# Probabilities times values: one full-array matmul per head pair in place of two column-tiled ones

## The chip, the core and the metric

The kernel runs on one core of a Trainium2 chip. Its engines are TensorE (PE; its weight loads are listed apart as PEld), VectorE (DVE), ScalarE (ACT), GpSimd (POOL) and SyncE (SP), which run side by side and wait for each other on semaphores. The metric is the device time of one execution in microseconds, less is better; the profile's own clock runs from the first instruction to the last and is called the span.

## What is computed

Two transformer blocks over 512 tokens of width 1024, batch 1, in float32. Two of their parts matter here.

The first block holds a sparse attention with 8 heads of width 64. An indexer chooses 128 keys for each query; the softmax runs over those alone. In the kernel the choice is a bias row (0 or a huge number), so that the products are dense:

```python
logits = jnp.einsum('bqhd,bqkhd->bqhk', qb, kg).astype(jnp.float32) * att_scale
p = jax.nn.softmax(logits, axis=-1).astype(v.dtype)
return jnp.einsum('bqhk,bqkhd->bqhd', p, vg)
```

The second block holds an attention with 8 query heads in 2 groups of 4, each group with one key and one value head of width 64. Its output is a gated sum of three branches: over compressed blocks (32 of them, the last one empty), over selected blocks and over a window. With 512 tokens the last two are plain causal attention with their own keys and values. Beside it stands a gated linear attention (GLA); both go through one output projection (`w_out_2`).

## The kernel before

**Precision.** The large projections (lines 298 to 300, in `mm3`) split both operands into a high and a low part in the type float32r and multiply three times. The attentions' score products of the second block use float32r too; the first block's score products, both blocks' products of probabilities and values, and the retention use plain float32. In the trace each plain float32 matmul is two records, a float32r matmul or a transpose is one.

**An attention** is built by `attend` (line 422): for a tile `t` of 128 queries and each of 4 head pairs `j` it returns three stages. `qk` makes the scores of both heads (line 842 in the first block, 1231 in the second) into PSUM tiles `ps_at` (2 buffers), then takes the row minimum on DVE (439), the exponential on ACT (442) and scales on DVE (449). `tp` transposes the probabilities on PE (419) into `ps_tr` (2 buffers) and copies them on ACT (457) to `pt`. `out` (line 463) multiplies: for each block `cc` of 128 keys and each head `a` of the pair, 64 columns of values are the weights and the 128 transposed probabilities stream past them. Head 0 of the pair uses columns 0 to 63 of PE's array and head 1 columns 64 to 127: two column tiles, listed as `128*64`. Matmuls that use the whole array are listed as `128*128`, those with 64 rows of the array, as line 842's, as `64*128`.

The result of a query tile, `pv()[feature, pair, q]` for all four pairs, fills one PSUM bank (`ps_pv`, one buffer). In the first block, `dsa` (833) copies it to `qaT` in one instruction on ACT (848). In the second, `nsa` (1219) collects three branches in it, the compressed one (`compressed`, line 1283: four matmuls for each query tile with block-diagonal weights `vblk`) and two calls of `attend`, and `split` (360, 361) then writes its high part on ACT and its low part on DVE over the queries, `qS`.

**The order.** `pipeline` (469) runs the stages of the items so that each item's `qk` comes two steps before its `out`. These steps are one task, and `tick` interleaves tasks with the projections: `dsa` runs beside the retention and its projections, `nsa` beside the GLA and its projections. The engines' instruction order is then made by the framework's scheduler from a timeline that it simulates; only in a stretch around lines 666 to 671 is PE's order as written. Each engine runs its list in order.

Of the kernel before, what the change touches and what calls it, by code (L numbers as in the profile page):

```python
# [14 lines left out]
P = 128  # L15
S = 512
# [9 lines left out]
# columns of the packed per-feature vectors  # L26
# [9 lines left out]
# columns of the packed shape-only constants  # L36
# [63 lines left out]
def _layout(inp):  # L100
# [58 lines left out]
    o["wo2"] = tiles(a["w_out_2"][0], KD)  # L159
# [5 lines left out]
class Builder:  # L165
    def __init__(self, nc, tc, ins, out, cdec, dbg=None):
# [5 lines left out]
        self.deep = (4, 3)   # buffers of the attentions' probabilities, and of their transposes  # L172

    # ---------------------------------------------------------------- small helpers
# [32 lines left out]
    def drain(self, t):  # L207
        """the rest of a task"""
# [5 lines left out]
    def tick(self):  # L214
        """emits a share of the work that goes on beside the projections"""
# [31 lines left out]
    def plan(self):  # L247
        """the pieces of the weights in the order of their use"""
# [23 lines left out]
    def ahead(self, n):  # L272
        """starts the next pieces of weights, so that n are ready or on their way"""
# [4 lines left out]
    def load(self, src, pool=None, eng=None):  # L278
        """a piece [128, a, b] of a weight -> its high and low part"""
# [25 lines left out]
    def projA(self, keys, act, ts=slice(0, S)):  # L305
        """out[f, tok] for 128 features, from one or several pieces of k tiles"""
# [19 lines left out]
    def projM(self, keys, act):  # L326
        """projA of three pieces of 8 k tiles, the first half of the tokens before the second"""
# [12 lines left out]
    def projB(self, name, ch, act, evac):  # L340
        """out[tok, n] for a chunk of columns; evac(tok, psum)"""
# [21 lines left out]
    def rsq(self, out, src, scale):  # L363
        """out = (src * scale + eps) ** -0.5 for a few columns"""
# [6 lines left out]
    def tok_sum(self, acc, name):  # L371
        """sums over the features of acc[f, tok] -> [128 tok, 4]"""
# [9 lines left out]
    def bcast(self, col, out):  # L382
        """[128 tok, 4] -> [128, 512], the same in every partition"""
# [20 lines left out]
    def rope(self, x, cos, sin, half, tmp, eng):  # L404
        """rotates x[p, h, 2 * half] in place; sin carries the sign of the first half"""
# [15 lines left out]
    # ---------------------------------------------------------------- attention  # L421
    def attend(self, t, pv, score, vtok, bias, first, rowscale=None):
        """softmax(q k) v of the 8 heads for the queries of tile t, added to pv()[feature, pair, q], as a list of
        stages per head pair. score(psum, h, n) puts out the negated, scaled products with the first n keys"""
# [3 lines left out]
        for j in range(4):  # L428
            Pm, PT, box = [], [], []

            def qk(j=j, Pm=Pm, box=box):
                sm = self.small.tile([P, 2], F32, name="sm", tag="sm", bufs=3)
                for a in range(2):
                    h = 2 * j + a
                    sc = self.ps("at")
                    score(sc, h, n)
# [9 lines left out]
                if rowscale is not None:  # L446
                    nc.vector.tensor_tensor(rs, rs, rowscale(2 * j), op=ALU.mult)
# [3 lines left out]
            def tp(Pm=Pm, PT=PT):  # L451
                for a in range(2):
# [16 lines left out]
    def pipeline(self, items):  # L469
        """the stages of the items, each one item behind the one before"""  # L470
# [16 lines left out]
    # ---------------------------------------------------------------- the whole  # L487
# [67 lines left out]
    def mod_rest(self, lo, hi):  # L555
        """the feature tiles lo .. hi of the modulation"""
# [29 lines left out]
    def norm2(self, acc, ts):  # L586
        """rms(x) * w * (1 + scale) + shift of the tokens ts, split"""
# [20 lines left out]
    # ---------------------------------------------------------------- first block: mixer  # L608
# [109 lines left out]
    def index_proj(self, qi, s0, mods):  # L718
        """the index queries, key and weights; all tiles of tokens grow together, as the feature tiles of h come in"""
# [31 lines left out]
    def index_scores(self, qi, scs):  # L751
# [4 lines left out]
        for t in range(NT):  # L756
# [5 lines left out]
            # the key: high part twice, low part twice; the queries: high and low part of each head  # L762
# [33 lines left out]
    def topk(self, scs):  # L796
        """the 128 largest of each row -> 0, the others -> BIG"""
# [35 lines left out]
    def dsa(self, qaT, kaT, va, scs, tiles):  # L833
        nc = self.nc
        items = []
        for t in tiles:
            bias = self.c("bigmask", 384, 512) if t == 0 else scs[t]
            pv = self.bank()
# [657 lines left out]
```

## Time and profile before

| | |
|---|---|
| median of 3 runs | 1640.35 us (1640.23 to 1642.13) |
| span of the profiled execution | 1638.9 us |
| PE busy | 1600.4 us, 98% of the span |
| PEld, DVE, ACT, POOL busy | 82%, 60%, 43%, 10% |
| granted TensorE clock, mean | 0.996 |
| first attention's line 463 | from 177.8 to 332.2 us |
| second attention's line 463 | from 1054.0 to 1217.2 us |

The profiled execution is one execution; the page gives its span and no time beside it, and the span is 1.45 us under the median of the runs. Matmuls are pipelined, so a record of a matmul is longer than the time that it takes from the next one: what a stretch of matmuls costs is read from where it starts and where the next one starts.

### The profile page before, as it was taken

The page shows a single profiled execution, that of the slowest core. Times are in us where ns is not written, and L with a number is a line of the kernel's source. Part 1 is how long each engine was busy: PE and PEld are TensorE (multiplying, and loading weights), DVE is VectorE, ACT ScalarE, POOL GpSimd, SP SyncE. Part 2 cuts the span into 40 slices and gives each one's busy share as a digit, 9 for nine tenths or more (in the row PEclk, how much of TensorE's full clock was granted, in tenths as well). Part 3 has the DMA queues.
Part 4 walks back from the last instruction along what each step waited for, and adds up shares of the span by engine and source line. Part 5 has one row for each costly group of instructions (what it writes and reads, how often), then busy time and mean ns, then how long its engine had stood idle before and what let it go on. Part 6 is the DMA issues. An engine that isn't in the chain of part 4 may idle for free.

```text
span 1638.9 us, 23692 instructions
## 1 busy us (share of the span) xinstructions
PE 1600.4 (98%) x8941; PEld 1347.3 (82%) x8941; DVE 979.3 (60%) x2233; ACT 696.6 (43%) x1476; POOL 170.1 (10%) x310
## 2 busy tenths in 40 slices
PE   4999999999999999999999999999999999999999
PEld 3899888887888988888888899977778788888887
DVE  7679755557886864443334455675666677777321
ACT  4563656634222642322333334654653444444221
POOL 4431000021110110000000015100110000000000
PEclk9999999999999999999999999999999999999999
DMA  8222221145553633333233353121013222222331
GB/s 320 89 85 90 78 65 40 52 135 180 181 183 118 184 119 123 116 115 104 87 106 108 120 165 98 52 67 50 14 52 103 81 99 90 102 91 87 109 111 53
DMA packets 49297, 173.12 MB, mean 106 GB/s; under 512 B 6032, under 2 KB 6592, under 8 KB 48160
## 3 DMA queue, kind: packets, MB, share of 16 engines
q1 hardware_dynamic: 43232, 152.22, 29.1%
q0 software_dynamic: 5952, 19.40, 3.5%
q8 instruction: 70, 1.15, 0.3%
q14 instruction: 43, 0.35, 0.1%
HBM read 166.88 MB, written 4.19 MB: 104 GB/s over the span
## 4 chain that ended last, share of the span: by engine, by line
PE 96%; DVE 3%; DMA 1%; ACT 0%; issue 0%; POOL 0%; SPq 0%; DVEq 0%; ACTq 0%; POOLq 0%
PE ps_mm L298 27%; PE ps_mm L299 27%; PE ps_mm L300 27%; PE ps_tr L419 4%; PE ps_pv L463 3%; DVE wacc L531 1%; PE ps_at L1231 1%; PE ps_at L842 1%; PE ps_at L1180 1%; PE ps_at L784 1%; PE ps_at L917 0%; PE ps_at L1251 0%; DMA xs<-in_x_dram 0%; PE ps_mm L1413 0%; PE ps_mm L1407 0%
## 5 line engine op out<-in xcount | busy, mean ns | idle before, releaser
L292 ACT CAST wh<-st 128x512 fp32r<-128x512 f32 (+3 forms) x508 | 283.8, 607 | 556.2 <-issue 273.8
L293 DVE TENSOR_TENSOR wl<-st,wh 128x512 fp32r<-128x512 f32 (+3 forms) x502 | 321.3, 670 | 179.5 <-ACT wh L292 178.5
L298 PE MATMUL ps_mm<-hH,wh 128*128 128x512 f32 (+1 forms) x1000 | 393.9, 395 | 4.2 <-DVE us L1458 2.2
L299 PE MATMUL ps_mm<-hL,wh 128*128 128x512 f32 (+1 forms) x1000 | 390.1, 390 | 0.3 <-DVE hL L361 0.3
L300 PE MATMUL ps_mm<-hH,wl 128*128 128x512 f32 (+1 forms) x1000 | 389.0, 389 | 0.0
L298 PEld LDWEIGHTS ps_mm<-hH,wh 128*128 128x128 f32 x1000 | 189.3, 189 | 44.4 <-DVE us L1458 2.4
L300 PEld LDWEIGHTS ps_mm<-hH,wl 128*128 128x128 f32 x1000 | 189.0, 189 | 41.1
L299 PEld LDWEIGHTS ps_mm<-hL,wh 128*128 128x128 f32 x1000 | 189.4, 189 | 38.7 <-DVE hL L361 0.5
L298 PE MATMUL ps_mm<-wh,hH 128*128 128x256 f32 (+2 forms) x672 | 195.9, 294 | 2.5 <-ACT hH L547 2.5
L299 PE MATMUL ps_mm<-wl,hH 128*128 128x256 f32 (+2 forms) x672 | 192.2, 288 | 0.0
L300 PE MATMUL ps_mm<-wh,hL 128*128 128x256 f32 (+2 forms) x672 | 189.2, 287 | 0.2 <-POOL hL L549 0.2
L298 PE MATMUL ps_mm<-fH,wh 128*128 128x512 f32 x352 | 138.8, 394 | 0.0
L299 PE MATMUL ps_mm<-fL,wh 128*128 128x512 f32 x352 | 138.7, 394 | 0.0
L300 PE MATMUL ps_mm<-fH,wl 128*128 128x512 f32 x352 | 138.5, 393 | 0.0
L298 PEld LDWEIGHTS ps_mm<-wh,hH 128*128 128x128 f32 x672 | 127.5, 190 | 4.8 <-ACT hH L547 2.5
L299 PEld LDWEIGHTS ps_mm<-wl,hH 128*128 128x128 f32 x672 | 127.7, 191 | 0.7 <-issue 0.2
L300 PEld LDWEIGHTS ps_mm<-wh,hL 128*128 128x128 f32 x672 | 126.4, 190 | 0.6 <-POOL hL L549 0.3
L580 DVE SCALAR_TENSOR_TENSOR ma<-ms,silu_c,ma 128x128 f32<-128x128 f32 x224 | 77.3, 348 | 5.2
L298 PEld LDWEIGHTS ps_mm<-fH,wh 128*128 128x128 f32 x352 | 66.3, 188 | 15.4
L300 PEld LDWEIGHTS ps_mm<-fH,wl 128*128 128x128 f32 x352 | 66.1, 188 | 15.6
L299 PEld LDWEIGHTS ps_mm<-fL,wh 128*128 128x128 f32 x352 | 66.2, 188 | 15.1
L442 ACT ACTIVATE pm<-lt,mn 128x128 f32<-128x128 f32 (+3 forms) x96 | 53.7, 560 | 23.1 <-DVE mn L439 22.5
(374 smaller groups left out, 2284.8 us busy)
## 6 DMA issues: line engine op xcount, KB each, us to landing
st<-in_wup_dram SPq DMA_DIRECT2D x44, 512.0 KB, 3.2
ms<-in_wada_dram POOLq DMA_DIRECT2D x64, 256.0 KB, 3.4
st<-in_wo_dram SPq DMA_DIRECT2D x24, 512.0 KB, 3.6
st<-in_wfg_dram SPq DMA_DIRECT2D x22, 512.0 KB, 3.5
st<-in_wfu_dram SPq DMA_DIRECT2D x22, 512.0 KB, 3.6
wa<-in_wada_dram SPq DMA_DIRECT2D x8, 1024.0 KB, 9.0
st<-in_wret_dram SPq DMA_DIRECT2D x16, 512.0 KB, 3.6
st<-in_wfd_dram SPq DMA_DIRECT2D x16, 448.0 KB, 3.2
```

The costliest lines, as they stand in the source:

```text
L292: nc.scalar.copy(hi[:, x0:x1], st[:, x0:x1])
L293: (eng or nc.vector).tensor_tensor(lo[:, x0:x1], st[:, x0:x1], hi[:, x0:x1].bitcast(F32), op=ALU.subtract)
L298: mm(ps, lh, rh, start=start, stop=False)
L299: mm(ps, lh, rl, start=False, stop=False)
L300: mm(ps, ll, rh, start=False, stop=stop)
L419: self.nc.tensor.transpose(out, src, self.c("ident", 0, n)[0:n])
L442: nc.scalar.activation(pm[:, 0:n], lt[:, 0:n], AF.Exp, bias=mn, scale=-1.0, accum_out=sm[:, a:a + 1])
L463: nc.tensor.matmul(pv()[a * 64:a * 64 + 64, j, :], vtok(cc, 2 * j + a), PT[a][:, cc * P:(cc + 1) * P], start=first and j == 0 and cc == 0, ...
L531: nc.vector.scalar_tensor_tensor(acc[:, h, :], w[:, kk, :], sc[:, kk:kk + 1], acc[:, h, :], op0=ALU.mult, op1=ALU.add)
L580: nc.vector.scalar_tensor_tensor(acc, w[:, k, :], s, acc, op0=ALU.mult, op1=ALU.add)
L784: nc.tensor.matmul(ps[:, 0:n], qS[:, h, :], ikS[:, i, 0:n], start=(i == 0), stop=(i == 1))
L842: nc.tensor.matmul(sc[:, 0:n], qaT[rows, h // 2, ts], kaT[rows, h // 2, 0:n], start=True, stop=True)
```

## The change

A pair's two heads are multiplied together: for each block of keys one matmul has 128 columns of values as weights (both heads') and streams the probabilities of both heads, 256 columns, over the whole array. Of the 128 x 256 results the halves where a head's values met its own probabilities are used; the other halves are left in PSUM. So a PSUM bank now holds two pairs, and a query tile fills the bank twice (`hf` 0 and 1), each time with its own evacuation, in two instructions on each engine with 64 partitions each.

In the second block a pair becomes heads `j` and `j + 4`, one of each group, so that the 128 columns of `vt` of a branch are the weights. The order of items per query tile changes from compressed, 4 pairs of a branch, 4 of the other to: compressed, 2 pairs of each branch, evacuation, an item that only has the second half of the compressed output, the other 2 pairs of each branch, evacuation. The compressed branch streams its transposed probabilities twice (a broadcast operand of 256 columns), with one 128 x 128 weight tile per pair, `vblk[:, j, :]`. The rows of `w_out_2` are permuted on the host to match. `pt` becomes one tile of both heads with 2 buffers (before: single tiles, 3 of them in the first block and 4 in the second); the compressed branch has its own tile `ptc`.

```diff
-    o["wo2"] = tiles(a["w_out_2"][0], KD)
+    w = a["w_out_2"][0]
+    o["wo2"] = tiles(np.concatenate([w[:512].reshape(2, 4, 64, D).transpose(1, 0, 2, 3).reshape(512, D), w[512:]]), KD)
...
-        self.deep = (4, 3)
+        self.deep = (4, 2)
...
-    def attend(self, t, pv, score, vtok, bias, first, rowscale=None):
+    def attend(self, t, js, heads, pv, score, vpair, bias, first, rowscale=None):
...
-        for j in range(4):
+        for i, j in enumerate(js):
...
             def tp(Pm=Pm, PT=PT):
+                pt = self.wa.tile([P, 2, S], F32, name="pt", tag="pt", bufs=self.deep[1])
                 for a in range(2):
                     tr = self.ps("tr")
                     for cc in range(t + 1):
                         self.transpose(tr[:, cc * P:(cc + 1) * P], Pm[a][:, cc * P:(cc + 1) * P])
-                    pt = self.wa.tile([P, S], F32, name="pt", tag="pt", bufs=self.deep[1])
-                    nc.scalar.copy(pt[:, 0:n], tr[:, 0:n])
-                    PT.append(pt)
-
-            def out(j=j, PT=PT):
+                    nc.scalar.copy(pt[:, a, 0:n], tr[:, 0:n])
+                PT.append(pt)
+
+            def out(i=i, j=j, PT=PT):
                 for cc in range(t + 1):
-                    for a in range(2):
-                        nc.tensor.matmul(pv()[a * 64:a * 64 + 64, j, :], vtok(cc, 2 * j + a), PT[a][:, cc * P:(cc + 1) * P],
-                                         start=first and j == 0 and cc == 0, stop=(cc == t), skip_group_check=True)
+                    nc.tensor.matmul(pv()[:, i], vpair(cc, j), PT[0][:, :, cc * P:(cc + 1) * P],
+                                     start=first and i == 0 and cc == 0, stop=(cc == t), skip_group_check=True)
...
-                box.append(self.ps("pv").rearrange("p (j q) -> p j q", q=P))
+                box.append(self.ps("pv").rearrange("p (j a q) -> p j a q", a=2, q=P))
...
-            items += self.attend(t, pv, score, lambda cc, h: va[:, cc, h * 64:(h + 1) * 64], bias, True)
-            def done(f=items[-1][2], pv=pv, t=t):
-                f()
-                nc.scalar.copy(qaT[:, :, t * P:(t + 1) * P], pv())
-            items[-1][2] = done
+            for hf in range(2):
+                pv = self.bank()
+                items += self.attend(t, (2 * hf, 2 * hf + 1), lambda j: (2 * j, 2 * j + 1), pv, score, lambda cc, j: va[:, cc, j * P:(j + 1) * P], bias, True)
+                def done(f=items[-1][2], pv=pv, t=t, hf=hf):
+                    f()
+                    for a in range(2):
+                        rows = slice(a * 64, a * 64 + 64)
+                        nc.scalar.copy(qaT[rows, 2 * hf:2 * hf + 2, t * P:(t + 1) * P], pv()[rows, :, a, :])
+                items[-1][2] = done
...
-        self.deep = (6, 4)
+        self.deep = (6, 2)
...
+            pvs = [self.bank(), self.bank()]
+            cmp = self.compressed(t, ts, pvs, qS, kc, vblk, gt)
...
+            for hf, pv in enumerate(pvs):
+                items.append([cmp[0], cmp[1], cmp[2]] if hf == 0 else [lambda: None, lambda: None, cmp[3]])
+                for br in range(2):
...
+                    items += self.attend(t, (2 * hf, 2 * hf + 1), lambda j: (j, j + 4), pv, score,
+                                         lambda cc, j, br=br: vt[:, cc, br * P:(br + 1) * P],
+                                         bias, False, rowscale=lambda j, br=br, t=t: gt[:, t, 1 + br, j:j + 5:4])
+                def done(f=items[-1][2], pv=pv, ts=ts, hf=hf):
+                    f()
+                    for a in range(2):
+                        rows = slice(a * 64, a * 64 + 64)
+                        self.split(pv()[rows, :, a, :], qS[rows, 2 * hf:2 * hf + 2, ts], qS[rows, 4 + 2 * hf:6 + 2 * hf, ts])
+                items[-1][2] = done
...
-        def out():
-            for j in range(4):
-                nc.tensor.matmul(pv()[:, j, :], vblk[:, j // 2, j % 2, :], box[1][:, (j // 2) * P:(j // 2 + 1) * P],
+        def out(hf):
+            for j in range(2):
+                nc.tensor.matmul(pvs[hf]()[:, j], vblk[:, j, :], box[1][:, hf * P:(hf + 1) * P].unsqueeze(1).to_broadcast([P, 2, P]),
                                  start=(j == 0), stop=False, skip_group_check=True)
```

## Rows read from the trace of the kernel before

**Rows 1.** The profile page: span, and chain that ended last by engine, by line.

```profile
span 1638.9 us, 23692 instructions
...
PE 96%; DVE 3%; DMA 1%; ACT 0%; issue 0%; POOL 0%; SPq 0%; DVEq 0%; ACTq 0%; POOLq 0%
PE ps_mm L298 27%; PE ps_mm L299 27%; PE ps_mm L300 27%; PE ps_tr L419 4%; PE ps_pv L463 3%; DVE wacc L531 1%; PE ps_at L1231 1%; PE ps_at L842 1%; PE ps_at L1180 1%; PE ps_at L784 1%; PE ps_at L917 0%; PE ps_at L1251 0%; DMA xs<-in_x_dram 0%; PE ps_mm L1413 0%; PE ps_mm L1407 0%
```

**Rows 2.** Busy time by stretch: bounds, length, then us busy (instructions) per engine.

```profile
280.00:320.00 40.00, 40.00 (x273) 31.88 (x271) 20.32 (x56) 22.91 (x46) 2.98 (x6) 1.00 0.17 53
1200.00:1222.00 22.00, 20.20 (x167) 15.04 (x164) 17.15 (x38) 11.61 (x25) 1.62 (x4) 1.00 0.29 96
```

**Rows 3.** Line 463 by operation: count; shortest, median, longest record in ns.

```profile
L463 PE MATMUL ps_pv<-pt,vt x320: 272/273/323, 1054.0 to 1217.2; 128*64 128x128 f32 x160
...
L463 PE MATMUL ps_pv<-pt,va x160: 272/273/324, 177.8 to 332.2; 128*64 128x128 f32 x160
```

**Rows 4.** Timeline of PE: start, length in us, engine, line; two groups.

```profile
1053.99 0.44 PE L463 MATMUL ps_pv<-pt,vt 128*64 128x128 f32 x4
1054.36 0.33 PE L419 MATMUL ps_tr<-cst,pm 128*128 128x128 f32 x1
...
308.21 1.13 PE L842 MATMUL ps_at<-kaT,qaT 64*128 64x512 f32 x4
309.27 1.09 PE L463 MATMUL ps_pv<-pt,va 128*64 128x128 f32 x16
310.29 1.09 PE L419 MATMUL ps_tr<-cst,pm 128*128 128x128 f32 x8
```

**Rows 5.** Timeline of PE, late in the second attention, as in group 4.

```profile
1203.19 0.43 PE L463 MATMUL ps_pv<-pt,vt 128*64 128x128 f32 x2
1203.56 0.66 PE L419 MATMUL ps_tr<-cst,pm 128*128 128x128 f32 x4
1204.14 1.09 PE L463 MATMUL ps_pv<-pt,vt 128*64 128x128 f32 x14
```

**Rows 6.** Timeline of PE in the retention: full-array matmuls of 256 columns.

```profile
339.81 0.59 PE L916 MATMUL ps_tr<-rv,rkd 128*128 128x256 f32 x2
340.24 0.59 PE L917 MATMUL ps_at<-rv,rinn 128*128 128x256 f32 x2
```

**Rows 7.** Timeline of PE: the compressed branch's matmuls of 128 columns.

```profile
1051.88 1.05 PE L1283 MATMUL ps_pv<-pt,vblk 128*128 128x128 f32 x8
1052.77 0.38 PE L419 MATMUL ps_tr<-cst,pm 128*128 128x128 f32 x2
```

**Rows 8.** Timeline of PE: first and last group of line 463, first attention.

```profile
177.79 0.43 PE L463 MATMUL ps_pv<-pt,va 128*64 128x128 f32 x2
...
331.79 0.66 PE L463 MATMUL ps_pv<-pt,va 128*64 128x128 f32 x8
```

**Rows 9.** Timeline of PE: score products of a pair that were placed apart.

```profile
286.99 1.12 PE L842 MATMUL ps_at<-kaT,qaT 64*128 64x512 f32 x2
...
288.62 1.12 PE L842 MATMUL ps_at<-kaT,qaT 64*128 64x512 f32 x2
```

**Rows 10.** Timeline of all engines: the bank handed over between two query tiles.

```profile
1186.01 0.58 ACT L360 CAST qS<-ps_pv 128x512 fp32r<-128x512 f32 x1 [1.80 <-PE ps_pv L463]
1186.62 0.69 DVE L361 TENSOR_TENSOR qS<-ps_pv,qS 128x512 fp32r<-128x512 f32 x1 [1.37 <-ACT qS L360]
...
1189.15 1.06 PE L1283 MATMUL ps_pv<-pt,vblk 128*128 128x128 f32 x8
```

**Rows 11.** Timeline of all engines: from the second attention to the output projection.

```profile
1216.39 1.09 PE L463 MATMUL ps_pv<-pt,vt 128*64 128x128 f32 x14 [0.37 <-ACT pt L457]
1217.51 0.58 ACT L360 CAST qS<-ps_pv 128x512 fp32r<-128x512 f32 x1 [1.18 <-PE ps_pv L463]
...
1218.15 0.96 PE L298 MATMUL ps_mm<-qS,wh 128*128 128x512 f32 x3 [0.67 <-ACT qS L360]
...
1218.95 0.43 PE L299 MATMUL ps_mm<-qS,wh 128*128 128x512 f32 x1
```

More of the change, by code (lines that the diff above doesn't have):

```diff
@@ L433, in qk @@
                 for a in range(2):
-                    h = 2 * j + a
                     sc = self.ps("at")
-                    score(sc, h, n)
+                    score(sc, heads(j)[a], n)
                     lt = self.wa.tile([P, S], F32, name="lt", tag="lt", bufs=2)
@@ L446, in qk @@
                 if rowscale is not None:
-                    nc.vector.tensor_tensor(rs, rs, rowscale(2 * j), op=ALU.mult)
+                    nc.vector.tensor_tensor(rs, rs, rowscale(j), op=ALU.mult)
                 for a in range(2):
@@ L837, in dsa @@
             bias = self.c("bigmask", 384, 512) if t == 0 else scs[t]
-            pv = self.bank()
             def score(sc, h, n, ts=slice(t * P, (t + 1) * P)):
@@ L1004, in block2_mix @@
         kc = b2.tile([P, 64], F32, name="kc")
-        vblk = b2.tile([P, 2, 2, P], F32, name="vblk")
+        vblk = b2.tile([P, 2, P], F32, name="vblk")
         nc.gpsimd.memset(vblk, 0.0)
@@ L1215, in compress @@
                     nc.tensor.matmul(o[:, 0:64], hid[:, m, g].rearrange("p a n -> p (a n)"), w2[:, 2 + m, :], start=(m == 0), stop=(m == 1))
-                for a in range(4):
-                    nc.vector.tensor_copy(vblk[a * 32:a * 32 + 32, g, a // 2, (a % 2) * 64:(a % 2) * 64 + 64], o[a * 32:a * 32 + 32, 0:64])
+                for a in (g, 2 + g):
+                    nc.vector.tensor_copy(vblk[a * 32:a * 32 + 32, a // 2, g * 64:g * 64 + 64], o[a * 32:a * 32 + 32, 0:64])
     def nsa(self, qS, kS, vt, kc, vblk, gt):
@@ L1223, in nsa, with score, compressed @@
             ts = slice(t * P, (t + 1) * P)
-            pv = self.bank()
-            items.append(self.compressed(t, ts, pv, qS, kc, vblk, gt))
+            pvs = [self.bank(), self.bank()]
+            cmp = self.compressed(t, ts, pvs, qS, kc, vblk, gt)
             bias = self.c("bigmask", 384 - t * P, 512)
-            for br in range(2):
-                def score(sc, h, n, br=br, ts=ts):
-                    n = max(n, 256)
-                    for i in range(2):
-                        nc.tensor.matmul(sc[:, 0:n], qS[:, h, ts], kS[:, i, 2 * br + h // 4, 0:n], start=(i == 0), stop=(i == 1))
-                items += self.attend(t, pv, score,
-                                     lambda cc, h, br=br: vt[:, cc, br * P + (h // 4) * 64:br * P + (h // 4) * 64 + 64],
-                                     bias, False, rowscale=lambda h, br=br, t=t: gt[:, t, 1 + br, h:h + 2])
-            def done(f=items[-1][2], pv=pv, ts=ts):
-                f()
-                self.split(pv(), qS[:, 0:4, ts], qS[:, 4:8, ts])
-            items[-1][2] = done
+            for hf, pv in enumerate(pvs):
+                items.append([cmp[0], cmp[1], cmp[2]] if hf == 0 else [lambda: None, lambda: None, cmp[3]])
+                for br in range(2):
+                    def score(sc, h, n, br=br, ts=ts):
+                        n = max(n, 256)
+                        for i in range(2):
+                            nc.tensor.matmul(sc[:, 0:n], qS[:, h, ts], kS[:, i, 2 * br + h // 4, 0:n], start=(i == 0), stop=(i == 1))
+                    items += self.attend(t, (2 * hf, 2 * hf + 1), lambda j: (j, j + 4), pv, score,
[7 more added lines that the diff above has]
+                items[-1][2] = done
         return self.pipeline(items)
-    def compressed(self, t, ts, pv, qS, kc, vblk, gt):
+    def compressed(self, t, ts, pvs, qS, kc, vblk, gt):
         nc = self.nc
@@ L1249, in qk @@
             sc = self.ps("at")
-            for h in range(8):
-                nc.tensor.matmul(sc[:, h * 32:(h + 1) * 32], qS[:, h, ts].bitcast(F32), kc[:, (h // 4) * 32:(h // 4) * 32 + 32],
+            for i in range(8):
+                h = i // 2 + (i % 2) * 4
+                nc.tensor.matmul(sc[:, i * 32:(i + 1) * 32], qS[:, h, ts].bitcast(F32), kc[:, (h // 4) * 32:(h // 4) * 32 + 32],
                                  start=True, stop=True)
@@ L1266, in qk @@
             nc.vector.reciprocal(rs, sm)
-            nc.vector.tensor_tensor(rs, rs, gt[:, t, 0, :], op=ALU.mult)
+            nc.vector.tensor_tensor(rs.rearrange("p (j g) -> p j g", g=2), rs.rearrange("p (j g) -> p j g", g=2),
+                                    gt[:, t, 0, :].rearrange("p (g j) -> p j g", g=2), op=ALU.mult)
             nc.vector.tensor_tensor(p3, p3, rs.unsqueeze(2).to_broadcast([P, 8, 32]), op=ALU.mult)
@@ L1276, in tp @@
                 self.transpose(tr[:, g * P:(g + 1) * P], box[0][:, g * P:(g + 1) * P])
-            pt = self.wa.tile([P, S], F32, name="pt", tag="pt", bufs=self.deep[1])
-            nc.scalar.copy(pt[:, 0:256], tr[:, 0:256])
+            pt = self.wa.tile([P, 256], F32, name="ptc", tag="ptc", bufs=2)
+            nc.scalar.copy(pt, tr[:, 0:256])
             box.append(pt)
-        def out():
-            for j in range(4):
-                nc.tensor.matmul(pv()[:, j, :], vblk[:, j // 2, j % 2, :], box[1][:, (j // 2) * P:(j // 2 + 1) * P],
+        def out(hf):
+            for j in range(2):
+                nc.tensor.matmul(pvs[hf]()[:, j], vblk[:, j, :], box[1][:, hf * P:(hf + 1) * P].unsqueeze(1).to_broadcast([P, 2, P]),
                                  start=(j == 0), stop=False, skip_group_check=True)
-        return [qk, tp, out]
+        return [qk, tp, lambda: out(0), lambda: out(1)]
     def gla_decay(self, q, glr, wg2, us):
```

## The prediction

> **What bounds the kernel now.** I read the page first. PE carries 96% of the chain that ended last, and line 463, the one that changes, is 3% of the span on that chain, some 49 us [rows 1]. The table by stretch then shows whether PE has slack where that line runs: in the first attention none (40.00 us busy of 40.00), at the end of the second 1.8 us in 22 [rows 2]. PE's clock is granted in full in both (1.00), so no term comes from it. The reader is to see that the change is paid or earned in PE's own instruction stream, as the sum of what each group of matmuls takes from its start to the next group's start; a shorter wait on another engine earns little. The length of a record is no help: line 463's take 273 ns each [rows 3], but many lie on top of each other.
>
> **What line 463 costs now.** It is 480 records, two per matmul [rows 3]. The timeline gives two lengths of a whole group: 4 records (one key block, both heads, two records each) take 1054.36 - 1053.99 = 0.37 us, 16 records (four key blocks) 310.29 - 309.27 = 1.02 us [rows 4]. So a key block streams in (1.02 - 0.37) / 3 = 0.217 us, and a group pays 0.15 us apart from that. The neighbours pay as well: four transposes between two such groups take 1204.14 - 1203.56 = 0.58 us [rows 5], while eight full-array records of the same size take 1052.77 - 1051.88 = 0.89 us, 0.111 each [rows 7], which makes 0.44 for four. Another 0.14. I charge 0.15 us for every change between array shapes, two per group, 0.30.
>
> The gain of two heads side by side needs both heads' matmuls next to each other. Where the scheduler cut a pair's list so that one head's two records stood alone, these cost 1203.56 - 1203.19 = 0.37 us [rows 5], as much as both heads' four.
>
> Counting the groups of line 463 along the whole timeline: 25 in the first attention [rows 8], with 8 groups of 2 records, 2 of 4, 5 of 6, 4 of 8, 3 of 10, 1 of 12 and 2 of 16; and 58 in the second, from the one in [rows 4] to the one in [rows 11], with 29 of 2, 5 of 4, 8 of 6, 8 of 10, 7 of 14 and 1 of 16. With every cut block rounded up that is 48 and 106 blocks, where 40 and 80 would do. Cost now: first attention 48 x 0.217 + 25 x 0.30 = 17.9 us; second 106 x 0.217 + 58 x 0.30 = 40.4 us.
>
> **What it costs after.** Half as many records, 80 and 160, each with 256 columns over the whole array. The retention has that very form: two records take 340.24 - 339.81 = 0.43 us, 0.215 each [rows 6]. A cut list loses nothing now, and next to other full-array matmuls no shape changes. Some changes stay, because the neighbour itself uses half the rows: on the timeline 18 of the 25 groups follow a score product of line 842 and 4 precede one, and in the second attention 7 follow a matmul of the GLA or a transpose with another shape. First attention: 80 x 0.215 + 22 x 0.15 = 20.5 us, that is +2.6. Second: 160 x 0.215 + 7 x 0.15 = 35.5 us, that is -4.9.
>
> The compressed branch keeps its 32 records but streams 256 columns in place of 128: 32 x (0.215 - 0.111) = +3.3 us [rows 6, 7].
>
> The Trainium skill's "TensorEngine Tiling (Array Packing)", section Theoretical Speedup, speaks against this change: operands of at most 64 columns gain up to twice from column tiling, so giving it up should double this work. By that rule alone, with nothing else charged, the 120 key blocks go from 0.217 to 0.43 us, +25.6 us, against the -2.3 us of my two sums. The same page's Key Properties say that a change of tiling mode drains the engine, and the 0.15 us above is this trace's size of that.
>
> **Evacuation.** The bank `ps_pv` is filled 16 times and not 8, with one buffer. A handover in the second attention takes ACT 0.58 us and then DVE 0.69 us, from 1186.01 to 1187.31, and the next matmul into the bank came at 1189.15, with 1.84 us to spare [rows 10]. After, two instructions on each engine have half the columns each; I take the same 1.3 us in all (an estimate from these rows; the trace has no such instruction). What hides it is the pipeline's other work on PE. Within a query tile there is less of it, since the item behind the handover has no scores and no transposes. So the four added handovers there cost between 0 and 4 x 1.3 = 5.2 us; the nearest row has slack, and I take 0.8. In the first attention the projections lie between: the bounds are the same, and I take 0.
>
> At the end, PE waits 0.67 us for the last evacuation before the output projection [rows 11]. After, the first two feature tiles of that projection come from the bank that was evacuated earlier, and their six matmuls cover the last one: -0.7 us; 0 if the scheduler puts others first.
>
> The larger `pt`, the buffers of `ptc`, four fewer copies into `vblk` and the added ACT and DVE instructions are costed at nothing: they lie on ACT and DVE, hidden behind PE, and in the busiest stretch DVE has 17.15 of 22 us [rows 2]. The permuted rows of `w_out_2` are the same bytes.
>
> **Sum.** +2.6 - 4.9 + 3.3 + 0.8 - 0.7 = +1.1 us on a span of 1638.9. The median of the runs is 1.45 us over that span, and the difference should stay: 1640.35 + 1.1 = 1641.5 us. About 0.2% (3.3 us, 1637.1 to 1643.6) is what a measurement of this kernel can tell from no change.
>
> **The bound that no row gives** is the new instruction order. It matters at line 842: two heads' score products next to each other take 1.13 us together at 512 columns [rows 4], one head's alone takes 1.12 [rows 9]. On the timeline five of the 16 pairs are apart, two with 512 columns and three with 384 (some 0.8 us each by the columns), 4.6 us in all. If the other eleven came apart as well, it would cost some 6.4 us by the same scaling.
>
> **Rivals.** (1) Faster: the new order keeps all pairs of line 842 together, because the products with the values no longer fit between the two heads. That takes away 4.6 us and five cuts with their two changes of shape, 1.5 us: 1635.4. For it: the cuts were made by groups of line 463. Against it: the second head waits for a `ps_at` buffer as before, and something else will fill that hole. (2) Slower: the handovers of `ps_pv` are bare. Eight added ones at 1.3 us are 10.4 in place of 0.8: 1651.1. It decides from about three bare ones on. For it: one buffer, and an item without cover behind it; against it: the 1.84 us to spare, and that nothing on PE waits for an evacuation but at the end. (3) Slower: the columns double and the 0.15 us do not go, because they belong to these matmuls and not to the shape. Then 83 x 0.30 - 29 x 0.15 = 20.6 us of my saving are not there: 1662. Against it: full-array groups of the same type stand 0.215 apart from their first record on [rows 6]. The tiling page's factor of two, named above, is what would rule here.
>
> **Chances.** The sum as it stands: 0.42. Rival 1: 0.30. Rival 2: 0.18. Rival 3: 0.06. The rest, 0.04, is spread by orders that I can't foresee. By the 0.2% bound: faster 0.31, same 0.43, slower 0.26. The likeliest case alone ranges from 1637 to 1646, by the handover's bounds and small changes of order. The range for 8 in 10 takes in rival 1 with a little more and rival 2 up to its full price: 1634 to 1652.
>
> **What would show it.** In the changed kernel's trace the products with values should be 240 records of form 128*128 with 256 columns, 0.215 us apart, and four transposes behind them should take 0.44 us, not 0.58. Of the first attention's 25 entries most should still show a late start behind line 842's products. The compressed records should stand 0.215 apart. The chain of waits should have no entry of PE behind the two evacuations' copies, and PE's 0.67 us before the output projection should be gone. Wrong would be the prediction if the transposes keep their 0.58 us, if `ps_pv`'s first matmuls wait for ACT or DVE more than twice, or if the score products' pairs are cut very differently from five in 16.

## The result, and the profile after

The changed kernel takes 1649.23 us (median of 4 runs, 1649.00 to 1649.75) against 1640.29 for the one before (4 runs): a ratio of 1.0051, 95% interval 1.0038 to 1.0064. It is slower by some 0.5%. The prediction had 1641.5; the time lies inside its range and 7.7 us from its number.

In the changed kernel the products with the values are line 464, the transposes 421, the compressed branch 1293, the scores of the first attention 842, the evacuation's cast and subtraction 362 and 363, the projection's three matmuls 300 to 302. The page, as in [rows 1]:

```profile
span 1646.9 us, 23191 instructions
...
PE 96%; DVE 3%; ACT 1%; issue 0%; DMA 0%; POOL 0%; SPq 0%; DVEq 0%; ACTq 0%; POOLq 0%
PE ps_mm L300 27%; PE ps_mm L301 27%; PE ps_mm L302 27%; PE ps_pv L464 3%; PE ps_tr L421 3%; DVE wacc L532 1%; PE ps_at L1237 1%; PE ps_at L842 1%; PE ps_at L1184 1%; PE ps_at L785 1%; PE ps_pv L1293 0%; PE ps_mm L1423 0%; PE ps_at L921 0%; PE ps_at L1260 0%; DMA xs<-in_x_dram 0%
```

PE still sets the end. The page tells no more than that, because the loss is spread over short stretches. The records of the products answer to [rows 3] (count; shortest, median, longest in ns; first and last start in us; form):

```profile
L464 PE MATMUL ps_pv<-pt,vt x160: 377/379/483, 1059.4 to 1227.1; 128*128 128x256 f32 x160
...
L464 PE MATMUL ps_pv<-pt,va x80: 377/379/483, 180.2 to 337.1; 128*128 128x256 f32 x80
```

Half as many, 240, each over the whole array with 256 columns. What a group costs is read from the timeline (start, length, engine, line, tiles, form, count, wait and what ended it):

```profile
300.98 1.12 PE L842 MATMUL ps_at<-kaT,qaT 64*128 64x512 f32 x2
302.03 1.56 PE L464 MATMUL ps_pv<-pt,va 128*128 128x256 f32 x6
303.52 1.12 PE L842 MATMUL ps_at<-kaT,qaT 64*128 64x512 f32 x2
...
1207.72 0.60 PE L421 MATMUL ps_tr<-cst,pm 128*128 128x128 f32 x4
1208.15 1.89 PE L464 MATMUL ps_pv<-pt,vt 128*128 128x256 f32 x8
1209.88 0.60 PE L421 MATMUL ps_tr<-cst,pm 128*128 128x128 f32 x4
...
1212.94 0.43 DVE L363 TENSOR_TENSOR qS<-ps_pv,qS 64x256 fp32r<-64x256 f32 x1
...
1213.52 1.04 PE L1293 MATMUL ps_pv<-ptc,vblk 128*128 128x256 f32 x4
...
1214.39 1.89 PE L464 MATMUL ps_pv<-pt,vt 128*128 128x256 f32 x8
```

Eight records take 1209.88 - 1208.15 = 1.73 us, 0.216 each; four of the compressed branch 0.87. Four transposes beside full-array neighbours take 1208.15 - 1207.72 = 0.43 us, where they took 0.58 [rows 5]. So the 0.15 us that a change of shape costs are gone where the shapes are now the same.

Then the span is cut at five starts on PE: the first score product of the first attention, the last transpose of the retention beside it, the first compressed score, the last matmul of the sum of squares behind the second attention and its output projection, and PE's last matmul. Behind that one come another 4.3 us in both kernels. The stages in us, each from the profiled execution:

| | start | first attention | middle | second attention and output projection | rest |
|---|---|---|---|---|---|
| before | 163.2 | 209.5 | 669.9 | 228.4 | 363.6 |
| after | 164.7 | 212.8 | 670.7 | 232.5 | 362.1 |
| difference | +1.5 | +3.3 | +0.8 | +4.1 | -1.5 |

But for the rounding, the differences have the sum of the spans' difference, +8.1.

**The start and the rest** cancel each other, and neither has anything of the change in it. PE's instructions are the same up to the first score product. Its clock is not. Busy time by stretch of the kernel before (bounds, length, busy us and instructions of PE, PEld, DVE, ACT and POOL, granted clock, DMA share, GB/s):

```profile
30.00:40.00 10.00, 6.39 (x25) 5.71 (x25) 9.93 (x15) 5.77 (x13) 5.89 (x4) 1.00 0.58 223
40.00:50.00 10.00, 9.34 (x57) 9.04 (x57) 9.75 (x12) 7.51 (x15) 7.73 (x5) 0.83 0.62 213
50.00:60.00 10.00, 6.79 (x41) 6.71 (x40) 8.83 (x19) 3.20 (x8) 1.77 (x3) 0.83 0.00 0
...
1276.00:1290.00 14.00, 11.82 (x49) 9.49 (x49) 8.13 (x14) 6.38 (x9) 0.00 (x0) 0.88 0.23 81
```

And of the changed kernel:

```profile
30.00:40.00 10.00, 4.86 (x24) 4.46 (x23) 9.93 (x15) 5.38 (x12) 5.95 (x4) 0.80 0.57 211
40.00:50.00 10.00, 10.00 (x55) 10.00 (x56) 9.34 (x13) 7.51 (x15) 7.28 (x5) 0.69 0.62 213
50.00:60.00 10.00, 7.20 (x33) 7.00 (x32) 8.69 (x18) 2.00 (x5) 1.97 (x2) 0.66 0.00 0
...
1226.00:1232.00 6.00, 3.07 (x12) 2.02 (x11) 3.34 (x6) 2.81 (x6) 0.13 (x2) 0.89 0.00 0
1232.00:1240.00 8.00, 8.00 (x32) 6.40 (x31) 2.98 (x5) 2.30 (x4) 0.00 (x0) 0.87 0.01 2
1240.00:1250.00 10.00, 10.00 (x45) 8.16 (x44) 6.98 (x12) 4.59 (x8) 0.00 (x0) 1.00 0.47 157
1276.00:1290.00 14.00, 14.00 (x69) 11.71 (x68) 3.63 (x9) 2.28 (x4) 1.21 (x2) 1.00 0.33 109
```

The start has a lower clock after, and around 1280 us it is the kernel before that loses 14 x 0.12 = 1.7 us. All eleven kernels of this study have such falls at the start and between 580 and 600 us. Six of them have one or two more, of some 1.7 us each, behind a wait or in mid-stretch and not always in the same place; I count these, where they fall, as a term of their own.

**The end of the second attention** is new. The timeline of all engines there, against [rows 11], with the first row that follows the evacuation's cast on ACT in the kernel before:

```profile
1217.99 2.19 ACT L360 CAST gH<-go 128x512 fp32r<-128x512 f32 x4
```

And in the changed kernel:

```profile
1212.48 0.72 PE L300 MATMUL ps_mm<-qS,wh 128*128 128x512 f32 x2
...
1227.47 0.37 ACT L362 CAST qS<-ps_pv 64x256 fp32r<-64x256 f32 x1 [2.08 <-PE ps_pv L464]
1227.74 2.17 ACT L362 CAST gH<-go 128x512 fp32r<-128x512 f32 x4
1227.87 0.42 DVE L363 TENSOR_TENSOR qS<-ps_pv,qS 64x256 fp32r<-64x256 f32 x1 [6.40 <-ACT qS L362]
1228.39 2.50 DVE L363 TENSOR_TENSOR gL<-go,gH 128x512 fp32r<-128x512 f32 x4
1229.94 0.37 ACT L362 CAST qS<-ps_pv 64x256 fp32r<-64x256 f32 x1
...
1230.36 1.35 PE L300 MATMUL ps_mm<-qS,wh 128*128 128x512 f32 x3 [2.93 <-ACT qS L362]
...
1231.99 0.63 PE L302 MATMUL ps_mm<-qS,wl 128*128 128x512 f32 x1
...
1232.42 0.63 PE L300 MATMUL ps_mm<-qS,wh 128*128 128x512 f32 x1
...
1234.60 0.39 PE L300 MATMUL ps_mm<-gH,wh 128*128 128x512 f32 x1
1234.83 0.39 PE L301 MATMUL ps_mm<-gL,wh 128*128 128x512 f32 x1
```

The last evacuation has two halves now, and the instruction order puts four casts of the GLA's output (2.17 us) between its two casts on ACT; before, the same four casts came behind the evacuation's only cast. There was a hole to put them in: in all eight evacuations of the changed kernel the second cast starts behind the first half's subtraction, and once ACT is seen to wait for it:

```profile
1078.90 0.37 ACT L362 CAST qS<-ps_pv 64x256 fp32r<-64x256 f32 x1 [0.41 <-DVE qS L363]
```

PE waits 2.93 us, where it waited 0.67. It has nothing left to fill the wait with: 18 matmuls of the output projection, six on the half that was evacuated earlier for each of three output tiles (`ps_mm` has three buffers), had already run between 1212.48 and 1222.44, among the last products with the values. The kernel before has none there. Behind the wait the projection's matmuls start 0.43 us apart (1231.99 to 1232.42), later 0.23 (1234.60 to 1234.83): the lower of the clock's two levels, 1.2 in place of 2.4 GHz. By the stretches above that is 6 x 0.11 + 8 x 0.13 = 1.7 us.

PE's waits over the whole span (us in total, times, longest), from the second attention on and one of the middle:

```profile
PE ps_mm L300 <- ACT qS L362: 2.9, 1, 2.9
...
PE ps_mm L300 <- DVE us L1468: 2.2, 1, 2.2
...
PE ps_pv L464 <- ACT pt L459: 0.7, 1, 0.7
PE ps_mm L300 <- ACT fs L962: 0.5, 1, 0.5
```

No wait of a first matmul into `ps_pv` is among them. The wait for `fs` in the middle is new: 0.5 of the middle's 0.8 us. Runs 1 and 2, which have the new first attention, show it too; runs 3 and 9, which have the old one, do not.

### The profile page after: what moved, and what is told of

The parts are those of the page before. It is cut to its first block, busy times and chain, and to the rows that moved or that the text cites. A ratio compares the mean times of both kernels' runs of the same rounds, so it can differ in the third digit from the quotient of the medians.

```text
span 1646.9 us, 23191 instructions
## 1 busy us (share of the span) xinstructions
PE 1606.0 (98%) x8701; PEld 1364.6 (83%) x8701; DVE 982.4 (60%) x2241; ACT 704.3 (43%) x1500; POOL 169.6 (10%) x310
## 4 chain that ended last, share of the span: by engine, by line
PE 96%; DVE 3%; ACT 1%; issue 0%; DMA 0%; POOL 0%; SPq 0%; DVEq 0%; ACTq 0%; POOLq 0%
PE ps_mm L300 27%; PE ps_mm L301 27%; PE ps_mm L302 27%; PE ps_pv L464 3%; PE ps_tr L421 3%; DVE wacc L532 1%; PE ps_at L1237 1%; PE ps_at L842 1%; PE ps_at L1184 1%; PE ps_at L785 1%; PE ps_pv L1293 0%; PE ps_mm L1423 0%; PE ps_at L921 0%; PE ps_at L1260 0%; DMA xs<-in_x_dram 0%
## 5 line engine op out<-in xcount | busy, mean ns | idle before, releaser
L444 ACT ACTIVATE pm<-lt,mn 128x128 f32<-128x128 f32 (+3 forms) x96 | 53.9, 561 | 32.3 <-DVE mn L441 31.8
```

The lines of the kernel that those rows point to most:

```text
L444: nc.scalar.activation(pm[:, 0:n], lt[:, 0:n], AF.Exp, bias=mn, scale=-1.0, accum_out=sm[:, a:a + 1])
```

## The experiments

**An account for the second attention.** All runs but run 8 are held against one sum, made with the prediction's prices: 0.215 us for a full-array record, 0.217 for a key block of column tiles, 0.15 for every change of array shape between one PE instruction and the next, and the difference of PE's waits and of the clock. Counts are by a walk over PE's instructions in the trace, from the first compressed score to the last product and the change of shape behind it: before, 105 key blocks with cut ones rounded up (106 in the prediction) and 171 changes of shape; PE idle 2.1 us, the output projection included. Difference to before, in us:

| kernel | streaming | compressed | changes of shape | idle | clock | sum | measured |
|---|---|---|---|---|---|---|---|
| after | +11.6 | +3.3 | 97 fewer: -14.6 | +1.8 | +1.7 | +3.8 | +4.1 |
| both attentions, casts together | +11.6 | +3.3 | 111 fewer: -16.7 | +2.0 | 0 | +0.2 | +0.3 |
| first attention alone | 0 | 0 | 0 | 0 | +1.7 | +1.7 | +1.8 |
| second alone | +11.6 | +3.3 | 97 fewer: -14.6 | +1.9 | +1.7 | +3.9 | +4.4 |
| column tiles kept | -1.1 | +3.3 | 23 fewer: -3.5 | +1.5 | +1.7 | +1.9 | +1.2 |
| second, casts together | +11.6 | +3.3 | 111 fewer: -16.7 | +1.7 | 0 | -0.1 | 0.0 |
| second, tiles, casts together | -0.9 | +3.3 | 15 fewer: -2.3 | +0.2 | 0 | +0.3 | +0.9 |
| the same, compressed as tiles | -0.4 | 0 | 4 fewer: -0.6 | +0.6 | 0 | -0.4 | +0.2 |
| second, last casts together | +11.6 | +3.3 | 97 fewer: -14.6 | -0.3 | 0 | 0.0 | +0.7 |

It holds within 0.7 us. The last row was forecast by the account before its run (+0.1); the others were made from the runs. Each row is one profiled execution, and executions of one kernel differ by more than these sums do (run 4: 1641.11 to 1646.51 us), so the ratios below come from all executions and the stages from one.

The same can be read without any price, as the time from each PE record's start to the next one's with the waits taken out. In the changed kernel the products of the second attention take 2.9 us more than before (31.8 to 34.7), the compressed branch 3.0 more, and the 168 transposes of the probabilities 4.7 less (21.1 to 16.5), with the same counts of transposes and compressed records. So the price of a shape change sits for the most part at the neighbours of the products.

**1. Casts together, in every evacuation.** The two casts of an evacuation come first, then the two subtractions (shortened: `high` and `low` stand for the slices of `qS`):

```diff
-    for a in range(2):
-        self.split(pv()[rows, :, a, :], high, low)
+    for a in range(2):
+        nc.scalar.copy(high, pv()[rows, :, a, :])
+    for a in range(2):
+        nc.vector.tensor_tensor(low, pv()[rows, :, a, :], high, op=subtract)
```

> The changed kernel with one edit: each evacuation of the second attention first writes the high parts of both halves on ACT, then both low parts on DVE. Theory (the last evacuation is cut in two and ACT does 2.17 us of other casts between its halves; PE then stands still for 2.93 us and its granted clock falls): the wait of PE before the output projection falls from 2.93 us to about 1, the clock stays full there, and the time goes from 1649.2 to 1645 to 1647 us. Rival (the time was lost before that point, and this wait only moves): PE's wait is shorter but the time stays within 1 us of 1649.2.

Measured: 1644.08 us, ratio 1.0018 (1.0010 to 1.0027), 0.9 us below the range that was expected. The wait at the end is 0.84 us and the clock stays at 1.00, as expected. The stage takes 228.7 in place of 232.5 us. But something else changed too: this order has 60 changes of shape against 74, and two bare handovers of the bank (0.31 and 1.26 us), which the changed kernel did not have. Its timeline of PE around the longer one:

```profile
1209.72 1.03 PE L421 MATMUL ps_tr<-cst,pm 128*128 128x128 f32 x8
1212.02 1.13 PE L1297 MATMUL ps_pv<-ptc,vblk 128*128 128x256 f32 x4 [1.26 <-DVE qS L1250]
```

So this run alone did not show what had brought the time back. Run 9 does.

**2 and 3. Each attention alone.** The first run has the old kernel's second attention and the new first one (`attend`, `bank` and `dsa` of the change); the second run the reverse.

> Only the first attention has the change; the second is that of the kernel before. Theory (PE's stream of the first attention grows by the doubled columns, of which the shape changes give back little, since most of them belong to the score products' half arrays): from the first score product to the end of the retention 3.3 us more, as in the changed kernel, and 1643 to 1645 us. Rival (the first attention is neutral, and what it seems to cost is the order of the instructions): within 1 us of 1640.3.

> Only the second attention has the change; the first is that of the kernel before. Theory (second attention: PE's stream about even, PE's wait of 2.9 us at its end and the clock's fall behind it): 1643 to 1646.5 us, with that wait still there. Rival (all of the loss lies in the second attention): 1648 to 1649 us. Second rival (the second attention gains, the first loses everything): at most 1640 us.

Measured: the first alone 1646.09 us, 1.0031 (1.0019 to 1.0042); the second alone 1643.90, 1.0019 (1.0010 to 1.0028). The parts add up to the whole, 0.31% and 0.19% against 0.51%. The first attention's stage is 212.8 in the one and 209.5 in the other, so its +3.3 us is its own. The first run came out 1.1 us above what was expected. Its profiled execution, the slowest of the six with 1647.64 us, shows the clock falling in the second attention, where nothing was changed:

```profile
1060.00:1070.00 10.00, 10.00 (x54) 7.72 (x53) 6.42 (x24) 4.64 (x16) 0.00 (x0) 0.83 0.00 0
```

10 x 0.17 = 1.7 us. It falls again behind the wait for `us`, as in the kernel before. Whether the other five executions have these falls is not known; the one with the highest mean clock, 0.996, took 1644.31 us. In the second run the long wait and the low clock behind it are both there (0.83 from 1220 to 1230 us).

**4. Column tiles kept in the new arrangement.** All of the change, but each key block is multiplied by two column-tiled matmuls of 64 columns again (shortened: `block` stands for `cc * P:(cc + 1) * P`):

```diff
-    nc.tensor.matmul(pv()[:, i], vpair(cc, j), PT[0][:, :, block], ...)
+    for a in range(2):
+        nc.tensor.matmul(pv()[a*64:a*64+64, i, a, :], vpair(cc, j)[:, a*64:a*64+64], PT[0][:, a, block], ...)
```

> The changed kernel with its banks, order, evacuations and compressed branch, but each pair's product is two column-tiled matmuls again, 64 columns of values and 128 probabilities each. Theory of the prediction (merging itself saves PE some 2 us in all, and the rest of the change costs): 1650 to 1653 us, the transposes behind the products back at 0.58 us for four. Rival (the doubled columns are what costs): 1640 to 1645 us.

Measured: 1643.85 us, 1.0015 (1.0007 to 1.0024), in the range of the rival and 6 us below that of the prediction's theory. The first attention takes 211.2 us, with one more of the score pairs cut, the second stage 229.6. What the prediction's theory said, that the full-array form pays in the second attention, is not seen in the time of this pair of kernels: with the same wait at the end, tiles are 2.9 us shorter there. By the account 1.9 of them are the tiles': 12.7 us less streaming, 11.1 more for changes of shape, 0.3 less waiting. Runs 5 and 6 below, the same pair without the long wait, have it the other way round: there the full-array form is the shorter by 0.9 us (228.4 and 229.3). So neither form is shown to win; which one is ahead turns on the order around it. The tiles' groups are cut less often in this arrangement than in the kernel before (23 changes of shape and 5 cut blocks less). The timeline shows the shape's price in place:

```profile
1201.19 0.66 PE L421 MATMUL ps_tr<-cst,pm 128*128 128x128 f32 x4
1201.78 0.43 PE L465 MATMUL ps_pv<-pt,vt 128*64 128x128 f32 x2
1202.14 0.66 PE L421 MATMUL ps_tr<-cst,pm 128*128 128x128 f32 x4
```

Four transposes take 0.59 us again, and a cut block 0.36.

**5 to 7. The second attention without the wait at its end.** All have the old first attention. Run 5 has the full-array products with the casts together; run 6 column tiles in their place; run 7 has the compressed branch in column tiles too, 128 columns for each head:

```diff
-    nc.tensor.matmul(pvs[hf]()[:, j], vblk[:, j, :], <256 columns, broadcast>, ...)
+    for a in range(2):
+        nc.tensor.matmul(pvs[hf]()[a*64:a*64+64, j, a, :], vblk[:, j, a*64:a*64+64], <128 columns>, ...)
```

> Only the second attention has the change, and both high parts of an evacuation come before both low parts. Theory (PE's stream of the second attention is even: 11.4 us more for the doubled columns, 3.3 more for the compressed branch, some 14.4 back for about 110 shape changes at 0.13 us): 1640 to 1642 us, no difference from the kernel before. Rival (the second attention was a gain that the wait at its end hid): 1636 to 1638 us. Second rival (something else in it costs): 1643 us or more.

> As the kernel with the second attention alone and the casts together, but with the pair's product as two column-tiled matmuls in the changed banks and order; the first attention is that of the kernel before. Theory (merging costs more than it gives, and the changed order cuts fewer pairs): the second attention to the end of its output projection takes 225 to 227 us, where the kernel before takes 228.4, and the whole 1637 to 1639.5 us. Rival (merging is worth its shape changes): 1641 us or more, slower than the merged form beside it.

> As the kernel with column tiles in the second attention, and the compressed branch's product as column tiles too, with 128 streamed columns per head and not 256 for both. Theory (the doubled columns of the compressed branch cost 3.3 us of PE, and its tiles stand beside others of the same shape): 3 us less than that kernel, 1634 to 1637 us. Rival (they lie in a stretch where PE has slack): no difference.

Measured: 1641.01 us, 0.9997 (0.9988 to 1.0006); 1640.87, 0.9996 (0.9987 to 1.0005); 1641.74, 1.0002 (0.9993 to 1.0010). Run 5 came as expected: the second attention costs as much as before. Runs 6 and 7 missed theirs: run 6 is 1.4 us above its range in time and its stage took 229.3 us in place of 225 to 227; run 7 is 4.7 us above its range. Run 6's expectation was made by taking the whole wait off run 4. In run 6 that wait fell from 2.92 to 0.83 us, but a bare handover of 0.87 came in and 8 more changes of shape; run 7 has 11 changes more than run 6 and two more cut blocks. Its time gives its rival's number, no difference, but not the rival's reason: the 3.3 us of the compressed branch did go, and by the account all but 0.7 of them came back as changes of shape, cut blocks and waits (the stage went from 229.3 to 228.6). In these orders, what one edit frees the next order partly takes back.

**8. The kernel before, heads one after the other.** Column tiles as before, but the loop over the heads is outside, so that the two heads' matmuls are not neighbours:

```diff
-    for cc in range(t + 1):
-        for a in range(2):
+    for a in range(2):
+        for cc in range(t + 1):
```

> The kernel before with one edit: all key blocks of the first head, then all of the second, so that two heads' matmuls rarely stand side by side. Theory (side by side they stream two heads in the time of one, 0.217 us per key block, and nothing else changes): 240 blocks in place of 154, 86 x 0.217 = 18.7 us more, 1657 to 1661 us. Since the products then stream as many columns as in the changed kernel, what it is slower than that kernel would be the price of the shape changes. Rival (the gain of two tiles is small, and the shape changes alone set the cost): less than 8 us more.

Measured: 1651.06 us, 1.0059 (1.0046 to 1.0072). Less than expected, since the instruction order still put some heads side by side: 53 of 172 steps of under 30 ns between records are left. For the same reason the price of the shape changes can't be read from it, as was planned. The rival, less than 8 us more, falls: it is 9.7. Its timeline of PE, where the kernel before has 1.02 us for such a group [rows 4]:

```profile
309.80 1.58 PE L463 MATMUL ps_pv<-pt,va 128*64 128x128 f32 x16
311.31 0.87 PE L419 MATMUL ps_tr<-cst,pm 128*128 128x128 f32 x6
```

1.51 us. So the gain of two tiles side by side is real, 0.49 us in a group of 16 records. The Trainium skill's "TensorEngine Tiling (Array Packing)", section Theoretical Speedup, says that narrow operands gain up to twice by column tiling. This trace agrees for the streaming: 1.73 us for four key blocks in the full-array form against 4 x 0.217 = 0.87.

**9. Casts together in the last evacuation alone.** Run 3 with run 1's edit where `ts.stop == S and hf == 1`, so that the order up to there stays.

> This kernel has the old first attention, and in the second one it puts the two casts together in the last evacuation alone; the other evacuations keep cast, subtraction, cast, subtraction. An account made from the earlier traces (columns streamed, 0.15 us for every change of array shape, PE's waits, the clock) gives the second attention with the output projection: streaming +11.6, compressed +3.3, 97 fewer changes of shape -14.6, PE's waits -0.2 (the wait at the end 0.84 us, no bare handover of the bank between the halves of the last query tile, where the kernel with all casts together waited 1.25 us). That is +0.1 us against before: a time of 1640 to 1642.5 us, a ratio of 0.9995 to 1.0008. The rival says that putting the casts together lowers the number of changes of shape by the new order and that this, not the shorter wait at the end, is what brought the time back: then the 97 changes remain here and so does 1.5 to 3 us of the loss: 1643 to 1645 us, with the clock's fall behind the output projection still there.

Measured: 1640.46 us, 1.0003 (0.9994 to 1.0012). The groups and the 74 changes of shape are those of run 3, so that the rival falls. Its end:

```profile
1222.29 0.75 ACT L1297 CAST qS<-ps_pv 64x256 fp32r<-64x256 f32 x2 [2.08 <-PE ps_pv L464]
1223.06 2.18 ACT L362 CAST gH<-go 128x512 fp32r<-128x512 f32 x4
...
1223.09 0.96 PE L300 MATMUL ps_mm<-qS,wh 128*128 128x512 f32 x3 [0.83 <-ACT qS L1297]
...
1224.32 0.39 PE L302 MATMUL ps_mm<-qS,wl 128*128 128x512 f32 x1
...
1224.55 0.39 PE L300 MATMUL ps_mm<-qS,wh 128*128 128x512 f32 x1
```

The wait is 0.83 us and the matmuls behind it are 0.23 us apart. The stage takes 229.05 us where run 3 took 232.81: 3.8 us less, of which 2.1 is the wait and 1.7 the clock. That one edit shows both to come from the order of the last evacuation's four instructions. The edit lifts two things at once, the second cast's place behind the first subtraction and the four casts in the hole. An estimate of their shares, from the changed kernel's rows: the first subtraction ended at 1227.87 + 0.42 = 1228.29 and the second cast started at 1229.94, so some 1.6 us of the wait are the four casts. In this run, too, the 18 matmuls of the projection run among the last products, and 0.83 us of wait stay. No version beat the kernel before by more than its interval.

## Why the prediction came out as it did

The prediction had PE's stream (both attentions' products with their changes of shape, and the compressed branch) at +1.0 us; by the stages and the account it is +3.6. It had the end at -0.7; that is +4.0, the wait and the clock. By its own steps:

- **Shape changes are paid by the shape, and stop with it: right.** Transposes 0.43 us, records 0.216 apart; rival 3, which had 1662, is refuted. The price of 0.15 us fits the second attention in nine kernels.
- **First attention, +2.6: measured +3.3.** The count was right (28 changes gone). The 0.7 us that are left over were not traced further.
- **Second attention, -4.9: by the account -3.0.** The streaming (+11.6) is as priced. The prediction took 109 changes away and 97 went: the 74 that are left are all at matmuls and transposes of the GLA (forms 64*64, 64*128 and two more), which the new order puts one by one between the full-array ones. The difference is 12 x 0.15 = 1.8 us. The order of run 1 has 111 fewer.
- **Compressed branch, +3.3: right.** Four records take 0.87 us.
- **Handovers, +0.8: 0 in this order, but once barely.** The last handover's subtraction ends at 1212.94 + 0.43 = 1213.37 and the next matmul into the bank starts at 1213.52, 0.15 us later. The estimate of 1.3 us for the evacuation's four instructions was too low: they take 1.75 to 4.9 us from the first cast to the last subtraction, since the halves go one behind the other and other work comes between. Run 1's order had the bank bare twice, 0.31 and 1.26 us. So rival 2's mechanism exists; here it did not bite.
- **End, -0.7: this is the step that failed.** The sum let six matmuls of the output projection, on the features evacuated earlier, cover the last evacuation, with a bound of 0 "if the scheduler puts others first". Two things went otherwise. The order ran these matmuls, 18 of them, among the last products, so that nothing was left to cover the evacuation. And ACT was given four casts of 2.17 us between the evacuation's two halves. The wait became 2.93, +2.3 us in place of -0.7, beyond the bound of 0, and the clock behind it lost 1.7 more. The prediction costed the added ACT and DVE instructions at nothing, as hidden behind PE; at the end nothing hid them. All other waits of PE in this stage together are 0.5 us shorter than before.
- **Score pairs: five of 16 apart, as before.** Two of the ten groups stand above (300.98 and 303.52). Rival 1 did not come about.
- **Not foreseen:** +0.8 in the middle, of which 0.5 is a new wait, and the clock's +1.5 at the start and -1.5 in the rest, which cancel here but can fall otherwise in any kernel.

In the second attention the miss is 4.1 + 1.5 = 5.6 us, against the prediction's -1.5 (-4.9 + 3.3 + 0.8 - 0.7): the waits 2.5 (+1.8 in place of -0.7), the shape changes 1.8, the clock 1.7, the streaming 0.2, the handover -0.8, and 0.2 without an account. The first attention adds 0.7 and the middle 0.8. The rest of the 7.7, some 0.7, lies outside the span. There the prediction's 1.45 us was too small: it set the median of some executions against the span of another. Every execution on record that has both its time and its span, of the kernel before too, is 2.0 to 2.2 us longer than its span.

That the time lies inside the range of 1634 to 1652 is luck. The likeliest case alone had 1637 to 1646, and the upper part stood for rival 2, bare handovers, of which there was none; a cause for which the range has no term brought the time there. Of the signs that the prediction named for being wrong (transposes at 0.58 us, first matmuls into `ps_pv` that wait, other cuts of the score pairs) none came. What it expected to see and did not come is that PE's 0.67 us before the output projection should be gone. The prediction asked no row which instructions could slip between the halves of an evacuation that is cut in two.

## What to carry to other kernels

Where column-tiled and full-array matmuls alternate in short groups, count the changes of shape: at 0.15 us each they weigh as much in the second attention here (14.6 us) as the doubled columns of products and compressed branch (14.9), so that one form or the other gains little, whichever it is. When an evacuation that PE waits for is cut into several instructions, look at what the order can put between them, and issue together the ones that PE needs first. And work that is meant to cover a wait covers it only if the order leaves it there. A longer stall of PE can cost more than its length: behind 2.9 us the matmuls here ran at the lower clock, behind 0.8 us they did not.

## What was not expected of the hardware

- Behind a wait of 2.92 or 2.93 us (after, runs 3 and 4) the 512-column matmuls ran 0.43 us apart for about 3 us; behind 0.67 to 0.84 us in the same place, in the other eight kernels, they ran 0.23 apart. That the longer wait brings the fall rests on these eleven traces, one execution each: three with the fall there, eight without. Between 1283 and 1294 us all kernels have the same wait of 2.2 us (for `us`), and behind it the clock fell in three of the eleven traces only, before, run 2 and run 7.
- The same instructions at the start ran with a granted clock of 0.66 to 1.00 between 30 and 60 us from kernel to kernel, which moved the first score product between 162.5 and 164.7 us. What sets it was not tried. For a change of a few us, that is as large as the effects in question.
